# State-space stage and gate projections of a hybrid decoder block: order written by hand instead of chosen by the scheduler

## The chip, the cores and the metric

One core of a Trainium2 chip runs the whole program. The metric is the device time of one execution in microseconds (us). Five engines take part, each with its own in-order instruction stream: TensorE (PE, matrix products and transposes), VectorE (DVE), ScalarE (ACT), GpSimd (POOL) and SyncE (SP, DMA issues). Engines wait for one another on semaphores only, so an instruction that waits holds everything behind it on its own engine.

## The reference

One decoder block on 512 tokens of width 1024. After a norm, one projection gives the inputs of a state-space (S5) branch `u`, of a sparse-attention branch, and two sets of gate inputs `g_ssm`, `g_attn` (1024 columns each):

```python
xn = rmsnorm(h, norm1_g[layer])
proj = xn @ w_in[layer]
u, q, k, v, qi, ki, wi, g_ssm, g_attn = jnp.split(proj, offsets, axis=-1)
y_ssm = s5_branch(u, ...)          # y = Re(C * scan(a_bar, b_bar u)) + d_skip*u; gelu; glu
y_attn = dsa_branch(q, k, v, qi, ki, wi)
merged = (sigmoid(g_ssm) * (y_ssm @ w_ssm_up[layer])
          + sigmoid(g_attn) * (y_attn @ w_attn_up[layer]))
h = h + merged @ w_out[layer]
h = h + peer_ffn(rmsnorm(h, norm2_g[layer]), ...)
return rmsnorm(h, norm_f_g)
```

The state of S5 is a complex number per group and state, so its rotation by time step stands in tables of cosines and sines. `peer_ffn` takes most of the time and is not touched.

## The kernel before, in words

**Products.** A float32 product is made of three float32r products of high and low parts (`mmh`, L245 to L250: wH by xH, wH by xL, wL by xH). A weight half (4 of the 8 row blocks of 256 columns) comes by one DMA (SP) into `wraw`, ACT casts its two 128x512 pieces to `wH` (L87), and POOL (in places DVE) subtracts to get `wL` (L88). So each half costs two L87 on ACT, two L88 on POOL and 24 products of 512 columns on PE. **Gates:** 2048 gate columns are 16 halves, 384 products `mm<-xnH,wH` and the like (loop at L668 to L680 in before): for every 256 columns two PSUM banks `mm`, then two ACT copies `mg<-mm` (L679) and two DMAs to `sig_d` in memory, from where they are read again when the branches are merged.

**S5.** 16 column groups are done in two halves of NQ = 8, each in two groups of four. `s5_tables` makes per half: the tables Ex on DVE (four products of 128x512 and four block-diagonal 64x512 operations), whose transposes ("turns", L580) PE puts into a PSUM bank and ACT copies out (L581); the rotation tables Rc, Rs by doubling from a first column, which POOL sets by two small memsets (L583, L584), seven levels of six DVE operations; the F tables (L137 on 128x640 and 64x640); the Br copies (L605); and the "direct" products L612 with ACT copies L617. `s5_main` then makes the "enter" products L634, turns the result by Rc, Rs on DVE (six operations of 128x512 per group), runs 16 scans (L645, L646), turns back (six more), makes the "sums" L656 to L659 (12 small products per group), adds `hf<-sp,hf` on DVE, and ACT takes 16 gelus per group (L666) into `yf`. L137 is the line of the helper through which all DVE tensor-tensor operations go; `hf` is the name of every S5 work tile. PSUM banks for S5 are `sp` and `po` only.

**Order.** In before, S5 and the gates stand in plain program order, and the tile scheduler places every instruction: it puts S5 table work on DVE into the gaps of the attention stage, 51 gate products ahead of attention, and the rest around the S5 products where PE would wait. Everything from the transposes of the attention output on (L688, `pt<-ident,yt`; then `yaH`, attn_up, glu, ssm_up, w_out, PEER) is the same in both kernels.

Of the kernel before, what the change touches and what calls it, by code (L numbers as in the profile page):

```python
# [59 lines left out]
def block_kernel(ctx, tc, I, out):  # L60
# [75 lines left out]
    def tt(o, a, b, op, e=V):  # L136
        e.tensor_tensor(o, a, b, op=op)  # L137
        return o
# [66 lines left out]
    with ExitStack() as fr:  # L205
# [6 lines left out]
        def mmps(tag="mm"):  # L212
            return psm.tile([P, 512], F32, name=tag, tag=tag, bufs=1 if tag == "sp" else 2)

        def tps():
            return pst.tile([P, 4, P], F32, name="pt", tag="pt")
# [116 lines left out]
        with tc.tile_pool(name="s5", bufs=1) as fp:  # L333
# [213 lines left out]
            Tq = half([NQ, P], "Tq")  # L547
            for z in (Fr, Fi, Tq):
                G.memset(z, 0.0)

            def s5ps(tag):
                ps = pso.tile([P, 4, P], F32, name="po", tag="po") if tag == "po" else mmps("sp")
                return ps if tag == "po" else ps.rearrange("p (x c) -> p x c", x=4)

            def s5_tables(q0):
                qs = slice(q0, q0 + NQ)

                def bc_s(a, n=4):
                    return a[:, qs, None, :].to_broadcast([P, NQ, n, 16])

                def bc_c(a, n=4):
                    return a[:, qs, :, None].to_broadcast([P, NQ, n, 16])

                def blockdiag(dst, a, b, op):
                    for j in range(2):
                        ps_ = slice(64 * j, 64 * j + 64)
                        tt(dst[ps_, :, :, 16 * j:16 * j + 16], a[ps_], b[ps_], op)

                ETr, ETi = half([NQ, P], "ETr"), half([NQ, P], "ETi")
                v1, v2 = half([NQ, 4, 16], "vr"), half([NQ, 4, 16], "vi")  # L570
                for part, dst in ((0, ETr), (1, ETi)):
                    Ex = half([NQ, 4, 32], "B" if part else "A")
                    G.memset(Ex, 0.0)
                    tt(v1, bc_c(rev_r), bc_s(bbi if part else bbr), ALU.mult)
                    tt(v2, bc_c(rev_i), bc_s(bbr if part else bbi), ALU.mult)
                    blockdiag(Ex, v1, v2, ALU.add if part else ALU.subtract)
                    for q in range(0, NQ, 4):
                        pt = s5ps("po" if q0 and q else "sp")
                        for x in range(4):
                            PE.transpose(pt[:, x, :], Ex[:, q + x].rearrange("p a b -> p (a b)"), ident)  # L580
                        S.copy(dst[:, q:q + 4, :], pt)  # L581
                Rc, Rs = half([NQ, P], "Rc"), half([NQ, P], "Rs")
                G.memset(Rc[:, :, 0:1], 1.0)  # L583
                G.memset(Rs[:, :, 0:1], 0.0)  # L584
                r1, r2 = half([NQ, 64], "D"), half([NQ, 64], "yk")
                n = 1
                for m in range(2, 9):
                    bc = lambda a: a[:, qs, None].to_broadcast([P, NQ, n])
                    cmul(Rc[:, :, n:2 * n], Rs[:, :, n:2 * n], Rc[:, :, :n], Rs[:, :, :n],
                         bc(zr[m]), bc(zi[m]), r1[:, :, :n], r2[:, :, :n])  # L590
                    n *= 2
                v1, v2 = half([NQ, 5, 16], "vr"), half([NQ, 5, 16], "vi")
                tt(v1, bc_c(ap_r, 5), bc_s(cr_, 5), ALU.mult)
                tt(v2, bc_c(ap_i, 5), bc_s(ci_, 5), ALU.mult)
                blockdiag(Fr, v1, v2, ALU.subtract)
                tt(v1, bc_c(ap_r, 5), bc_s(ci_, 5), ALU.mult)
                tt(v2, bc_c(ap_n, 5), bc_s(cr_, 5), ALU.mult)
                blockdiag(Fi, v2, v1, ALU.subtract)
                Brs = []
                for src, tg in ((bbr, "C"), (bbi, "A")):  # L600
                    Br = half([NQ, 4, 32], tg)
                    G.memset(Br, 0.0)
                    for j in range(2):
                        ps_ = slice(64 * j, 64 * j + 64)
                        V.tensor_copy(Br[ps_, :, :, 16 * j:16 * j + 16],  # L605
                                      src[ps_, qs][:, :, None, :].to_broadcast([64, NQ, 4, 16]))
                    Brs.append(Br)
                for q in range(0, NQ, 4):
                    pt = s5ps("po" if q0 and q else "sp")
                    for x in range(4):  # L610
                        for Br, Fx in zip(Brs, (Fr, Fi)):
                            PE.matmul(pt[:, x, :], Br[:, q + x].rearrange("p a b -> p (a b)"),  # L612
                                      Fx[:, q + x, 0:4, :].rearrange("p a b -> p (a b)"),
                                      start=(Br is Brs[0]), stop=(Br is Brs[1]))
                    for s in range(4):
                        ps_ = slice(32 * s, 32 * s + 32)
                        S.copy(Tq[ps_, q:q + 4, 32 * s:], pt[ps_, :, :P - 32 * s])  # L617
                return ETr, ETi, Rc, Rs

            yf = at.tile([P, 4, T], F32, name="yf", tag="qT")  # L620

            def s5_main(q0, tabs, uk):
                ETr, ETi, Rc, Rs = tabs
                vr, vi = half([NQ, P], "vr"), half([NQ, P], "vi")
                groups = [slice(q, q + 4) for q in range(0, NQ, 4)]
                HHr, HHi = half([NQ, P + 1], "A"), half([NQ, P + 1], "B")
                x1, x2 = half([NQ, P], "C"), half([NQ, P], "D")
                V.memset(HHr[:, :, 0:1], 0.0)
                V.memset(HHi[:, :, 0:1], 0.0)
                for g, gq in enumerate(groups):  # L630
                    pr, pi = s5ps("sp"), s5ps("po")
                    for ET, ps in ((ETr, pr), (ETi, pi)):
                        for x in range(4):
                            PE.matmul(ps[:, x], ET[:, 4 * g + x, :], uk[:, q0 + 4 * g + x, :], start=True, stop=True)  # L634
                    tt(x1[:, gq], pr, Rc[:, gq], ALU.mult)
                    tt(vi[:, gq], pr, Rs[:, gq], ALU.mult)
                    tt(vr[:, gq], pi, Rs[:, gq], ALU.mult)
                    tt(x2[:, gq], pi, Rc[:, gq], ALU.mult)
                    tt(x1[:, gq], x1[:, gq], vr[:, gq], ALU.add)
                    tt(x2[:, gq], x2[:, gq], vi[:, gq], ALU.subtract)  # L640
                yk = half([NQ, P], "yk")
                for n_, g in enumerate(groups):
                    for q in range(g.start, g.stop):
                        rb = r4[:, q0 + q:q0 + q + 1].to_broadcast([P, P])
                        V.tensor_tensor_scan(vr[:, q], rb, x1[:, q], 0.0, op0=ALU.mult, op1=ALU.add)  # L645
                        V.tensor_tensor_scan(vi[:, q], rb, x2[:, q], 0.0, op0=ALU.mult, op1=ALU.add)  # L646
                    tt(x1[:, g], vr[:, g], Rc[:, g], ALU.mult)
                    tt(x2[:, g], vi[:, g], Rs[:, g], ALU.mult)
                    tt(HHr[:, g, 1:], x1[:, g], x2[:, g], ALU.subtract)
                    tt(x1[:, g], vi[:, g], Rc[:, g], ALU.mult)  # L650
                    tt(x2[:, g], vr[:, g], Rs[:, g], ALU.mult)
                    tt(HHi[:, g, 1:], x1[:, g], x2[:, g], ALU.add)
                    ps = s5ps("po" if n_ else "sp")
                    for x in range(4):
                        q = g.start + x
                        PE.matmul(ps[:, x], Tq[:, q, :], uk[:, q0 + q, :], start=True, stop=False)  # L656
                        PE.matmul(ps[:, x], Fr[:, q, 1:5, :].rearrange("p a b -> p (a b)"), HHr[:, q, :P],
                                  start=False, stop=False)
                        PE.matmul(ps[:, x], Fi[:, q, 1:5, :].rearrange("p a b -> p (a b)"), HHi[:, q, :P],  # L659
                                  start=False, stop=True)  # L660
                    yq, uq = yk[:, g], uk[:, q0 + g.start:q0 + g.stop]
                    tt(yq, uq, dsk[:, q0 + g.start:q0 + g.stop, None].to_broadcast([P, 4, P]), ALU.mult)
                    tt(yq, ps, yq, ALU.add)
                    for m in range(4):
                        for x in range(4):
                            S.activation(yf[32 * m:32 * m + 32, (q0 + g.start) // 4, x * P:x * P + P],  # L666
                                         yq[32 * x:32 * x + 32, m, :], AF.Gelu_apprx_tanh)

            for q0 in range(0, 16, NQ):
                s5_main(q0, s5_tables(q0), uk)  # L670


            for side in range(2):
                for c0 in range(0, D, 256):
                    pss = [mmps(), mmps()]
                    ch_chunk(win, 1576 + D * side + c0, xnH, xnL, pss)
                    for c in range(2):
                        sg = mtile()
                        S.activation(sg, pss[c], AF.Copy)  # L679
                        S.dma_start(sig_d[8 * side + c0 // P + c], sg)  # L680

        lt = fr.enter_context(tc.tile_pool(name="late", bufs=1))
        yaH = lt.tile([P, 4, T], F32R, name="yaH", tag="aH")
# [770 lines left out]
```

## Time and profile before

| | us |
|---|---|
| three runs | 1655.98, 1655.98, 1665.59 (median 1655.98) |
| the profiled execution, own time | 1661.05 |
| its span in the trace | 1659.3 |
| PE busy in the span | 1596.2 (96%) |
| DVE busy | 1327.2 (80%) |
| ACT busy | 701.1 (42%) |
| POOL busy | 702.9 (42%) |

The page gives busy time per engine over the whole span. PE is the bound of the program as a whole, by the PEER stages behind about 430 us; the change lies between about 125 us and 314 us, and there the rows by stage are what counts. "Busy" of PE comes from modelled ends of pipelined products: products that follow one another every 0.23 us are each shown as 0.39 us long. A row of the timeline has its start, its duration, the engine, the line, the tiles and, in brackets, the idle time before it and what ended it.

### The profile page before, as it was taken

The numbers are of one execution on the slowest core, as the hardware profiler recorded it, in microseconds if no ns is written. First come the engines' busy times: TensorE is split into PE (matmuls) and PEld (weight loads), VectorE is DVE, ScalarE is ACT, GpSimd is POOL, SyncE is SP. The second block draws the span as 40 slices with busy tenths as digits, with TensorE's granted clock in tenths as the row PEclk, the third lists the DMA queues.
The fourth block names the chain that finished last, engine by engine and source line by source line (L and its number), as shares of the span: only waits on it lengthen the run. The fifth ranks groups of instructions, "written<-read, shape, count | busy, mean of one in ns | idle before, by whom it ended". The sixth has DMA issues, their size and how long they took to land.

```text
span 1659.3 us, 24741 instructions
## 1 busy us (share of the span) xinstructions
PE 1596.2 (96%) x8942; PEld 1385.5 (84%) x8942; DVE 1327.2 (80%) x2743; ACT 701.1 (42%) x1216; POOL 702.9 (42%) x520
## 2 busy tenths in 40 slices
PE   6899978999999999999999999999999999999997
PEld 5886766789888999888898878888899999999986
DVE  6997798262579998998757788888778888888886
ACT  5536453553443355456543333333333333333334
POOL 4440141444334557654374233233344445544450
PEclk9999999999999999999999999999999999999999
DMA  6151022534523468876689999999999999999994
GB/s 192 45 147 39 26 85 81 165 127 155 166 93 111 139 206 322 293 244 241 257 288 330 375 366 351 377 378 315 308 340 339 357 338 345 364 330 353 356 326 171
DMA packets 183563, 408.15 MB, mean 246 GB/s; under 512 B 15441, under 2 KB 100993, under 8 KB 180369
## 3 DMA queue, kind: packets, MB, share of 16 engines
q1 hardware_dynamic: 136640, 224.37, 40.3%
q0 software_dynamic: 39168, 142.62, 24.2%
q10 hardware_dynamic: 7632, 39.59, 5.9%
q8 instruction: 70, 1.15, 0.3%
q14 instruction: 53, 0.43, 0.1%
HBM read 361.09 MB, written 45.44 MB: 245 GB/s over the span
## 4 chain that ended last, share of the span: by engine, by line
PE 62%; DVE 17%; DMA 3%; issue 3%; ACT 2%; POOL 1%; SPq 0%; DVEq 0%; ACTq 0%; POOLq 0%
PE acc L1310 9%; PE acc L1309 9%; PE acc L1308 9%; PE pu L99 8%; PE pu L101 8%; PE pu L100 7%; DVE hf L137 3%; PE pg L1076 2%; DMA raw<-peer_v 2%; DVE ti L874 1%; DVE rows L1121 1%; DVE pr L137 1%; DVE tv L872 1%; PE mm L248 1%; PE mm L249 1%
## 5 line engine op out<-in xcount | busy, mean ns | idle before, releaser
L99 PE MATMUL pu<-hnH,eH 128*128 128x368 f32 x1024 | 354.4, 346 | 0.0
L101 PE MATMUL pu<-hnH,eL 128*128 128x368 f32 x1024 | 337.6, 330 | 0.0
L100 PE MATMUL pu<-hnL,eH 128*128 128x368 f32 x1024 | 337.5, 330 | 0.0
L87 ACT CAST eH<-raw 128x1024 fp32r<-128x1024 f32 (+1 forms) x290 | 285.9, 992 | 109.1 <-PE acc L1310 49.2
L88 DVE TENSOR_TENSOR eL<-raw,eH 128x1024 fp32r<-128x1024 f32 x185 | 226.5, 1225 | 100.9 <-ACT eH L87 99.2
L1310 PE MATMUL acc<-eH,AL 128*128 128x512 f32 x768 | 305.6, 398 | 0.3 <-DVE AL L137 0.3
L1309 PE MATMUL acc<-eL,AH 128*128 128x512 f32 x768 | 302.7, 394 | 0.0
L1308 PE MATMUL acc<-eH,AH 128*128 128x512 f32 x768 | 301.6, 393 | 0.1
L88 POOL TENSOR_TENSOR eL<-raw,eH 128x1024 fp32r<-128x1024 f32 (+1 forms) x105 | 215.3, 2061 | 199.8 <-ACT eH L87 197.9
L826 POOL DMA_INDIRECT rows<-peer_v,eid x128 | 164.2, 1282 | 238.1 <-DVE acc0g L840 213.7
L826 POOL DMA_INDIRECT rows<-peer_u,eid x128 | 159.6, 1247 | 197.1 <-DVE rows L838 180.5
L88 POOL TENSOR_TENSOR wL<-wraw,wH 128x512 fp32r<-128x512 f32 (+1 forms) x90 | 127.6, 1442 | 188.6 <-ACT wH L87 188.6
L100 PEld LDWEIGHTS pu<-hnL,eH 128*128 128x128 f32 x1024 | 193.6, 189 | 2.5
L99 PEld LDWEIGHTS pu<-hnH,eH 128*128 128x128 f32 x1024 | 193.2, 189 | 2.7
L101 PEld LDWEIGHTS pu<-hnH,eL 128*128 128x128 f32 x1024 | 193.1, 189 | 0.0
L838 DVE SCALAR_TENSOR_TENSOR rows<-rows,hn 128x1024 f32<-128x1024 f32 x128 | 168.6, 1319 | 19.9 <-DMA rows<-peer_u,eid 19.8
L1310 PEld LDWEIGHTS acc<-eH,AL 128*128 128x128 f32 x768 | 144.2, 188 | 34.5 <-DVE AL L137 1.2
L1309 PEld LDWEIGHTS acc<-eL,AH 128*128 128x128 f32 x768 | 144.1, 188 | 34.3
L1308 PEld LDWEIGHTS acc<-eH,AH 128*128 128x128 f32 x768 | 144.2, 188 | 32.3 <-ACT AH L1294 0.5
L840 DVE SCALAR_TENSOR_TENSOR acc0g<-rows,dots,acc0g 128x1024 f32<-128x1024 f32 x128 | 163.9, 1280 | 8.6 <-DMA rows<-peer_v,eid 8.1
L1294 ACT CAST AH<-am 128x384 fp32r<-128x384 f32 x128 | 65.8, 514 | 246.4 <-DVE am L137 244.7
L804 ACT ACTIVATE hg<-pu 128x368 f32<-128x368 f32 x56 | 26.8, 478 | 152.5 <-PE pu L101 152.5
(396 smaller groups left out, 2727.8 us busy)
## 6 DMA issues: line engine op xcount, KB each, us to landing
raw<-uT SPq DMA_DIRECT2D x128, 512.0 KB
raw<-peer_v SPq DMA_DIRECT2D x128, 512.0 KB
g_d<-stg ACTq DMA_DIRECT2D x24, 1024.0 KB
gt<-g_d SPq DMA_DIRECT2D x16, 1536.0 KB
wraw<-w_in SPq DMA_DIRECT2D x26, 512.0 KB
hold_d<-hold ACTq DMA_DIRECT2D x13, 768.0 KB
hold<-hold_d SPq DMA_DIRECT2D x13, 768.0 KB
raw<-peer_wq SPq DMA_DIRECT2D x16, 512.0 KB
```

Of the source, the lines that this page charges most:

```text
L87: S.copy(H, src)
L88: e.tensor_tensor(L, src, H.bitcast(F32), op=ALU.subtract)
L99: PE.matmul(ps, wh, xh, start=first, stop=False)
L100: PE.matmul(ps, wh, xl, start=False, stop=False)
L101: PE.matmul(ps, wl, xh, start=False, stop=last)
L137: e.tensor_tensor(o, a, b, op=op)
L826: G.indirect_dma_start(out=r, out_offset=None, in_=I["peer_v"] if tab else I["peer_u"], in_offset=bass.IndirectOffsetOnAxis(ap=eid[:, j:j ...
L838: V.scalar_tensor_tensor(r, r, 1.0, hn0, op0=ALU.mult, op1=ALU.mult, accum_out=dj)
L840: V.scalar_tensor_tensor(acc0, r, dj, acc0, op0=ALU.mult, op1=ALU.add)
L1308: PE.matmul(o, AH[:, ts], H[:, cs], start=st, stop=False)
L1309: PE.matmul(o, AH[:, ts], L[:, cs], start=False, stop=False)
L1310: PE.matmul(o, AL[:, ts], H[:, cs], start=False, stop=sp)
```

## The change

S5 and gates go into a block in which the scheduler moves nothing: the order on each engine is the order in which the code emits. A small planner in the code keeps two clocks (`pe`, `dve`) with assumed costs (0.69 for three gate products, 0.9 per turn, 1.8 per enter or direct, 2.7 per sums, 0.09 + n/800 per DVE operation) and puts gate steps of three products between S5 products until the PE clock is 2 us past the time at which the operands should be ready. The S5 tables of a half now stand as one piece ahead of its main part, both adds of a half stand behind all its scans, four banks instead of two take S5 products (`sp`, `po`, `pt`, `pt`), and gate banks alternate between `mm` and `as`. Gate weights are loaded two halves ahead; gelus are kept in `later` and emitted when the PE clock has passed their time. The products, DVE operations and gelus themselves are the same in kind and number.

```diff
+            class Gates:
+                def load(self):
+                    if self.todo:
+                        c0, k0 = self.todo.pop(0)
+                        self.W.append(whalf(win, k0, c0, 256))
+                def run(self):
+                    for n in range(8):
+                        tag = "as" if n % 2 else "mm"
+                        pss = [mmps(tag), mmps(tag)]
+                        for hf in range(2):
+                            H, L = self.W.pop(0)
+                            for c in range(2):
+                                for k in range(4):
+                                    mmh(pss[c], [...], hf == k == 0, hf == 1 and k == 3)
+                                    yield
+                                if hf:
+                                    sg = mtile()
+                                    S.activation(sg, pss[c], AF.Copy)
+                                    S.dma_start(sig_d[2 * n + c], sg)
+                            self.load()
...
+            def product(t, cost, fn):
+                while now["pe"] < t + 2.0:
+                    while later and later[0][0] <= now["pe"]:
+                        later.pop(0)[1]()
+                    if next(dense.steps, dense) is dense:
+                        break
+                    now["pe"] += 0.69
+                now["pe"] = max(now["pe"], t) + cost
+                fn()
...
+            banks = ["sp", "po", "pt", "pt"]
...
                 Rc, Rs = half([NQ, P], "Rc"), half([NQ, P], "Rs")
                 G.memset(Rc[:, :, 0:1], 1.0)
                 G.memset(Rs[:, :, 0:1], 0.0)
...
+                    product(now["dve"] - 1.0, 1.8, direct)
...
+                def leave():
+                    for g, yq, t in outs:
+                        ps = s5ps()
...
+                        product(t, 2.7, sums)
+                        t_ = vt(yq, ps, yq, ALU.add, now["pe"] + 0.3)
...
+                        later.append((t_ + 0.5, active))
...
-            for q0 in range(0, 16, NQ):
-                s5_main(q0, s5_tables(q0), uk)
-            for side in range(2):
-                for c0 in range(0, D, 256):
-                    pss = [mmps(), mmps()]
-                    ch_chunk(win, 1576 + D * side + c0, xnH, xnL, pss)
...
+            for _ in range(2):
+                dense.load()
+            now["dve"] = 0.0
+            with tc.manual_schedule():
+                for q0 in range(0, 16, NQ):
+                    tables = s5_tables(q0)
+                    ins = s5_enter(q0, next(tables))
+                    Rc, Rs = next(tables)
+                    s5_main(q0, ins, Rc, Rs)()
+                while next(dense.steps, dense) is not dense:
+                    now["pe"] += 0.69
+                    while later and later[0][0] <= now["pe"]:
+                        later.pop(0)[1]()
+                for _, fn in later:
+                    fn()
```

**POOL, the queue from the first S5 memsets on.** L88 is the subtraction for a weight's low part; L583 and L584 (before) and L641 and L642 (after) set the first column of Rc and Rs, on which the doubling of the rotations starts. Before:

```order
L573 MEMSET hf 128x1024
L88 TENSOR_TENSOR wL<-wraw,wH 128x512 x2
L573 MEMSET hf 128x1024
L602 MEMSET hf 128x1024
L88 TENSOR_TENSOR wL<-wraw,wH 128x512 x24
L602 MEMSET hf 128x1024
L88 TENSOR_TENSOR wL<-wraw,wH 128x512 x6
L583 MEMSET hf 128x8
L584 MEMSET hf 128x8
```

After:

```order
L635 MEMSET hf 128x1024
L88 TENSOR_TENSOR wL<-wraw,wH 128x512 x20
L641 MEMSET hf 128x8
L642 MEMSET hf 128x8
L694 MEMSET hf 128x1024 x2
L88 TENSOR_TENSOR wL<-wraw,wH 128x512 x12
L635 MEMSET hf 128x1024 x2
L88 TENSOR_TENSOR wL<-wraw,wH 128x512 x2
L641 MEMSET hf 128x8
L642 MEMSET hf 128x8
```

In before the first half's column memsets stand ahead of the weight splits; in after those of the first half stand behind 20 splits, of which the last two belong to a gate half, and those of the second half behind a gate half's pair again.

**ACT, around the first half's gelus.** `mg<-as` copies a gate bank out, L672 copies a turn out, L762 is the gelu. After:

```order
L87 CAST wH<-wraw 128x512 x4
L762 ACT_TABLE_LOAD
L762 ACTIVATE yf<-hf 32x128 x32
L579 ACTIVATE mg<-as 128x512
L580 DMA sig_d<-mg 128x512
L579 ACTIVATE mg<-as 128x512
L580 DMA sig_d<-mg 128x512
L87 CAST wH<-wraw 128x512 x2
L672 COPY hf<-sp 128x512
L672 COPY hf<-po 128x512
L672 COPY hf<-pt 128x512 x2
```

In before the gelus of the two groups stood apart, 16 and 16, with a gate copy and a weight cast between them; in after all 32 of a half stand together, and the weight casts (L87) whose splits come ahead of the second half's L641 stand behind them.

**ACT, the end of the stage.** The gelus of the last groups, the casts `ys<-yf` of the S5 output and the casts `yaH<-pt` of the attention output, after:

```order
L762 ACTIVATE yf<-hf 32x128 x16
L87 CAST wH<-wraw 128x512 x2
L762 ACTIVATE yf<-hf 32x128 x16
L87 CAST wH<-wraw 128x512
L87 CAST ys<-yf 128x512
L579 ACTIVATE mg<-as 128x512
L87 CAST ys<-yf 128x512
L580 DMA sig_d<-mg 128x512
L87 CAST ys<-yf 128x512 x2
L579 ACTIVATE mg<-as 128x512
L87 CAST yaH<-pt 128x4x128
```

In before the same gelus and `ys` casts are followed by four more gate copies `mg<-mm` with their weight casts before the first `yaH`; in after two gate copies are left there. On PE the pieces move the same way: 102 gate products stood between the last sums and the transposes L688, 36 do now; 24 instead of 51 stand ahead of attention.

## Rows read from the trace of the kernel before

**Rows 1.** Busy time of each engine by stage (windows view, core 0).
```profile
core 0: us, PE busy (x) PEld busy (x) DVE busy (x) ACT busy (x) POOL busy (x), PEclk, DMA share, GB/s
66.00:125.00 59.00, 55.99 (x338) 49.03 (x337) 58.91 (x182) 18.37 (x37) 24.76 (x19) 1.00 0.44 126
125.00:183.00 58.00, 57.13 (x327) 39.74 (x328) 44.99 (x214) 34.49 (x103) 3.53 (x3) 0.97 0.09 27
183.00:287.00 104.00, 84.82 (x471) 69.17 (x471) 92.33 (x167) 41.93 (x99) 32.00 (x24) 0.98 0.24 73
287.00:314.00 27.00, 24.45 (x110) 19.44 (x108) 6.08 (x6) 17.72 (x40) 12.57 (x9) 1.00 0.54 179
```
**Rows 2.** PE's waits, 183 to 313 us: total us, times, longest.
```profile
PE sp L657 <- DVE hf L137: 4.1, 2, 2.3
PE sp L612 <- DVE hf L137: 3.1, 2, 2.0
```
**Rows 3.** DVE's waits in the same stretch.
```profile
DVE hf L137 <- PE po L659: 4.7, 2, 4.0
```
**Rows 4.** DVE's timeline: the end of attention, the last S5 add.
```profile
181.82 0.69 DVE L137 TENSOR_TENSOR yt<-po,sums 128x512 f32<-128x512 f32 x1 [1.50 <-PE po L433]
...
286.63 0.69 DVE L137 TENSOR_TENSOR hf<-po,hf 128x512 f32<-128x512 f32 x1 [4.01 <-PE po L659]
```
**Rows 5.** PE's timeline: last sums' start, gate products behind the last sums, first attn_up product.
```profile
284.19 0.38 PE L659 MATMUL po<-hf 128*128 128x128 f32 x2
...
286.34 0.47 PE L250 MATMUL mm<-xnH,wL 128*128 128x512 f32 x1
...
311.74 0.39 PE L249 MATMUL mm<-xnL,wH 128*128 128x512 f32 x1
311.97 0.39 PE L250 MATMUL mm<-xnH,wL 128*128 128x512 f32 x1
...
316.51 0.74 PE L248 MATMUL mm<-yaH,wH 128*128 128x512 f32 x2 [0.67 <-ACT yaH L87]
```
**Rows 6.** Operations on S5 tiles in the attention stage: DVE's sum, then groups (ns min/median/max).
```profile
125.00:183.00 58.00, 20.75 (x56) 0.97 0.09 27
...
L137 DVE TENSOR_TENSOR hf<-hf x17: 169/284/690, 139.8 to 179.0; 64x512 f32<-64x512 f32 x4, 128x8 f32<-128x8 f32 x2, 128x16 f32<-128x16 f32 x2, 128x32 f32<-128x32 f32 x2
L137 DVE TENSOR_TENSOR hf<-sm,s_br x2: 418/419/420, 157.1 to 162.6; 128x256 f32<-128x256 f32 x2
...
L137 DVE TENSOR_TENSOR hf<-rev_r,bbr x1: 689/689/689, 165.5 to 165.5; 128x512 f32<-128x512 f32 x1
...
L137 DVE TENSOR_TENSOR hf<-ap_r,s_cr x1: 821/821/821, 178.1 to 178.1; 128x640 f32<-128x640 f32 x1
```
**Rows 7.** POOL by line, 183 to 287 us: count, busy us, mean ns, idle.
```profile
L88 POOL TENSOR_TENSOR wL<-wraw,wH 128x512 fp32r<-128x512 f32 x18 | 28.1, 1579 | 52.9 <-ACT wH L87 52.9
```
**Rows 8.** POOL's timeline: a pair of splits beside DVE, a single one.
```profile
210.84 3.65 POOL L88 TENSOR_TENSOR wL<-wraw,wH 128x512 fp32r<-128x512 f32 x2 [4.43 <-ACT wH L87]
...
274.02 1.27 POOL L88 TENSOR_TENSOR wL<-wraw,wH 128x512 fp32r<-128x512 f32 x1 [5.59 <-ACT wH L87]
```
**Rows 9.** DVE's timeline: the same operation beside a split and without one.
```profile
211.66 1.69 DVE L137 TENSOR_TENSOR hf<-hf 128x512 f32<-128x512 f32 x1
...
216.21 0.66 DVE L137 TENSOR_TENSOR hf<-hf 128x512 f32<-128x512 f32 x1
```
**Rows 10.** ACT's timeline: gelus, turn copies, weight casts, last casts of the stage.
```profile
232.41 0.59 ACT L581 COPY hf<-sp 128x512 f32<-128x512 f32 x1
...
287.35 5.10 ACT L666 ACTIVATE yf<-hf 32x128 f32<-32x128 f32 x16 [1.64 <-DVE hf L137]
292.48 0.60 ACT L679 ACTIVATE mg<-mm 128x512 f32<-128x512 f32 x1
...
294.14 1.14 ACT L87 CAST ys<-yf 128x512 fp32r<-128x512 f32 x2
...
313.23 0.58 ACT L87 CAST yaH<-pt 128x512 fp32r<-128x512 f32 x1
```

## What the time will be

> **What bounds the kernel now.** The page gives PE as the bound of the whole program, but the change lies in four stages, so I read busy time by stage first [rows 1]. Up to 125 us DVE has no room (58.91 of 59 us busy). In attention, to 183 us, PE has none (57.13 of 58). From 183 to 287 us, the S5 stage, neither is full: DVE 92.33 of 104, PE 84.82. From 287 to 314 us PE works off the rest of the gates. PE's waits say who is late in the S5 stage: sums and direct products waiting for DVE [rows 2]. DVE in turn waits longest for the very last sums, 4.0 us [rows 3], after which it has nothing to do in S5. So in before DVE sets the pace to 287 us and then PE does, with 102 gate products behind the last sums: they run from 286.34 to 312.2 us [rows 5]. At 316.51 us attn_up starts, and from there on both kernels run the same instructions on PE. A shift of that start is the change in time.
>
> **What PE gains.** Between 183 and 314 us PE is busy 84.82 + 24.45 = 109.3 of 131 us and idle 21.7. The changed kernel leaves 27 more gate products to this stretch (24 instead of 51 ahead of attention). One follows another in 0.23 us [rows 5], so that is 6.1 us more work. Nearly all 27 come out of the DVE-bound stage before 125 us, where they cost nothing; I count four inside attention, and taking these out lets attention end 0.9 us earlier. If PE then never waited, its stretch would end 21.7 - 6.1 + 0.9 = 16.5 us earlier. That is the most the change can give by this way.
>
> **What DVE must do.** DVE ends attention at 182.5 us and its last S5 add at 287.3 [rows 4]. Of these 104.8 us it works 92.33 + 0.9 (what lies outside the stage's window) = 93.2 and waits 11.6. Now its work grows. In attention it did 20.75 us of S5 work in gaps [rows 6]. Of this stay there: four Ex products of 0.69, four block-diagonal operations of 0.69 (the longest of their group), and the input matrix (four of 0.42 and two near 0.4): 8.0 us. The first half's rotations and two F products (0.82 each) go behind attention, as the emitted order has them: 20.75 - 8.0 = 12.8 us. They were hidden under a full PE; now nothing hides them. Without a single wait and with as many disturbances as before, DVE would end at 182.5 - 0.9 + 93.2 + 12.8 = 287.6, the same time as now. All that removing DVE's waits can give is used up by moving the rotations.
>
> **What is added to it.** Four terms:
>
> First, the wait for the first column. The doubling starts on a column that POOL sets, now behind a gate half's two splits, which stand behind their casts on ACT, which stand behind the copy of a turn. From the end of attention: copy 0.59 [rows 10], one cast 0.57 (half of the pair of 1.14), two splits of 1.27 each [rows 8]: 3.7, and 0.5 for the turn, 4.2 us. Some of it can lie before attention ends. I take 3.5, between 0 and 4.5.
>
> Second, the same in the second half, but behind gelus. From the first add on: 32 gelus 10.2, two gate copies 1.2, one cast 0.57, two splits 2.54 (sizes from [rows 8, 10]), 14.5 us to the memset. Meanwhile DVE waits some 1.5 us for the second sums, adds (0.69) and makes Ex (5.5): 7.7. The rest, 6.8, is a wait in which DVE has nothing: in its program the rotations come next. Behind DVE there wait F, Br, the direct products and all mains. I take 7; below 0 it cannot go, and above lies 9 if the copies wait for their gate products.
>
> Third, the adds. Both stand behind all scans, and the second one waits for its 12 products. Before, the last sums took from 284.19 to 286.34 us [rows 5], 2.2 us, while DVE has one add (0.69) to do: 1.5 us in each half, 3.0 us. In before the first add was hidden by the second group's scans. Between 1 and 4.
>
> Fourth, splits. A 128x512 operation that takes 0.66 us alone took 1.69 beside a split of POOL [rows 9], the split in the pair 1.83 instead of 1.27 [rows 8]: 1.03 us lost on DVE for each. The S5 stage had 18 of them [rows 7]; after, 14 halves of gate weights are cast and split behind attention and ahead of the last sums, since weights come two halves ahead: 28. Of the ten more, I take six to fall into DVE's waits (two ahead of each column memset, two in the waits at adds), so four by 1.03: 4.1 us, between 0 and 10.3.
>
> In the Trainium skill, page "SBUF — State Buffer", section "Who interferes with whom", a DVE instruction with two SBUF inputs contends with a GpSimd instruction that reads SBUF, as one holder at a time. Rotations have two SBUF inputs, so moving them out of attention, where POOL is busy 3.53 us, to where it splits weights speaks against this change. With a lock held for the split's whole 1.27 us the four would cost 5.1 instead of 4.1 us; the trace agrees with the rule in kind and shows somewhat less per split.
>
> DVE's last add is then at 287.6 + 3.5 + 7 + 3.0 + 4.1 = 305.2 us.
>
> **The tail.** Before, the last 16 gelus began at 287.35 us and were hidden by gate products; the `yaH` casts stood at 313.23 [rows 10]. Now 32 gelus come together. The first add is 1.5 + 0.7 us ahead of the second, so they start at 303.0; 32 take 10.2, a pair of casts between them 1.1: 314.3. Then come a cast 0.5, four `ys` casts 2.1 and two gate copies 1.2: the first `yaH` at 318.1 instead of 313.23, +4.9 us. PE, with only 36 gate products (8.2 us) behind the last sums, is ready before that: the cover of the gelus is gone. attn_up shifts by the same 4.9 us, from 316.5 to 321.4. Added to the profiled execution's own 1661.05 that is 1666; the runs' median is 5 us below this execution, so by it 1655.98 + 4.9 = 1661 us.
>
> **The rivals.**
>
> A: PE is the bound and the planner's cover works. For it: PE waits sum to 21.7 us, and gate steps in threes fit into them; four banks let it run ahead. It would need DVE's waits gone. With the first two terms and the splits at 0 and the adds at 1, DVE ends at 288.6, and the same 12.9 us from its last add to `yaH` give 301.5. PE has 109.3 + 6.1 - 1.8 (at most, what lies behind 312.2 is transposes) from 182.1 us on, to 295.7, and with some 3 us at the sums it ends near 299, so `yaH` rules: -11.7 us, 1644 us. Against it: the two column memsets stand in POOL's queue as written.
>
> B: the weights come late (slower). The casts ahead of the second column memset need their weights; if these are not there, the 6.8 us wait grows one for one, and all DVE work of the second half with it. It decides from 6.8 + 11.7 = 18.5 us of wait, when the whole is over 1% slower; with 20 us the time is 1655.98 + 4.9 + 13.2 = 1674 us. Against it: DMA engines are busy 0.24 of the stage [rows 1], and a load leaves two halves, 48 products or 11 us of PE, ahead.
>
> C: the change of order does nothing to the end. DVE was done at 287.3 us and PE at 312.2, 25 us of slack; if DVE's four terms come out at 13 instead of 17.6 us, its growth of 13 and the longer tail just fill that slack, and the first `yaH` stands where it stood: 0 to +1 us, 1656. For it: two of the terms rest on how POOL and ACT interleave, and may be smaller. Against it: each of them has its instructions in the emitted order.
>
> A lower clock is a doubt at both ends: the granted clock was 0.98 of full speed in the S5 stage and 0.97 in attention [rows 1], with PE at work 0.82 of the time in S5. With fewer gate products ahead of attention and longer PE waits at the sums it may fall once more, but while DVE sets the pace this lies beside it; 2 us at most in the tail.
>
> **How the numbers follow.** 1% is 16.6 us, about what a measurement of this kernel can tell from no change. Forecast (DVE chain with the tail) 0.55, with about 1655 to 1667 as its own range. C 0.13. A 0.20, a third of it beyond 1%, if the sums wait less than I give them and attention ends earlier still. B, with the upper ends of the four terms (305.2 + 1 + 2 + 1 + 6.2 = 315.4, so +15.1 us, 1671), 0.12, two thirds beyond 1%. Faster: 0.07 from A and 0.03 for a gain in attention that these rows do not show, 0.10. Slower: 0.08 from B and 0.04 from the forecast's own tail, 0.12. Within 1%: 0.78. The range reaches to A below, 1643, and to the upper ends above, 1672.
>
> **What would show it.** Right: attention's last DVE operation near 181 to 182 us, then a DVE gap of some 3 us before the first small rotation and one of some 7 us in the second half, both ended by POOL's memset; 32 gelus in a row; PE idle in front of the last transposes. The first term is wrong if the first rotation follows attention at once; the second if the memset L641 is done before Ex ends; the fourth if no more DVE operations of two SBUF inputs show 1 us on top beside a split than before. The tail is wrong if gate products still run when `yaH` starts. The whole is wrong if PE has fewer than 10 us idle from 183 us to the transposes.

## The result and the profile after

The changed kernel takes 1705.45 us (three runs, 1704.0 to 1706.29), the one before 1655.98 (1655.98 to 1665.59): 1.0275 times as long, with a 95% interval of 1.0252 to 1.0298 (the two medians alone stand at 1.030, since two of the three runs of before gave 1655.98). It is 2.75% slower; the prediction was 1661 us with a range of 1643 to 1672. The profiled execution of after has a span of 1703.7 us and a mean granted clock of 0.964 of full speed, before 0.992. (Some executions of e1 and e2 below ended 30 to 40 us later than the others of the same kernel; they are told there, since their cause is the subject here.)

Busy time by stage of the kernel after; it answers [rows 1], with the same columns.

```profile
core 0: us, PE busy (x) PEld busy (x) DVE busy (x) ACT busy (x) POOL busy (x), PEclk, DMA share, GB/s
66.00:125.00 59.00, 51.61 (x317) 45.38 (x315) 58.87 (x190) 16.43 (x35) 18.14 (x14) 0.97 0.38 108
125.00:183.00 58.00, 57.54 (x182) 37.56 (x180) 25.53 (x140) 20.98 (x71) 0.00 (x0) 0.50 0.00 1
183.00:240.00 57.00, 52.76 (x272) 41.05 (x271) 36.67 (x74) 20.28 (x42) 17.86 (x14) 0.91 0.20 57
240.00:287.00 47.00, 39.87 (x219) 35.14 (x220) 36.30 (x70) 23.16 (x57) 14.50 (x14) 0.89 0.22 67
287.00:314.00 27.00, 19.90 (x89) 16.18 (x87) 26.12 (x45) 7.40 (x13) 10.03 (x7) 0.91 0.50 156
314.00:411.00 97.00, 88.24 (x399) 73.52 (x400) 53.95 (x82) 50.82 (x104) 35.73 (x26) 0.92 0.36 117
```

The row to look at is the second. PE is shown as busy as before (57.54 of 58 us), but the granted clock is 0.50 (1.2 GHz) where it was 0.97, and 182 matmul records stand where there were 327. A PE column alone would not have shown it. PE's timeline ahead of attention and inside it, in after:

```profile
118.23 0.39 PE L250 MATMUL mm<-xnH,wL 128*128 128x512 f32 x1
124.33 1.00 PE L447 MATMUL as<-kT,qT 64*128 64x128 f32 x4 [5.71 <-DVE mx L450]
...
183.52 2.07 PE L447 MATMUL as<-kT,qT 64*128 64x512 f32 x2
...
191.07 1.12 PE L447 MATMUL as<-kT,qT 64*128 64x512 f32 x2
```

The 24 gate products end at 118.6 us; PE then has nothing until DVE's `mx` is there, 5.71 us, and no gate product stands inside attention. But for four scores that ran at 112.5 us, attention starts at the low clock and stays there: its scores of 64x512 take 2.07 us for a pair at 183.5 us, and 1.12 us only from about 190 us on.

DVE's timeline in after: the last operation of attention, the first rotation of each half, the second add of each half. It answers [rows 3, 4].

```profile
206.10 0.69 DVE L137 TENSOR_TENSOR yt<-po,sums 128x512 f32<-128x512 f32 x1 [2.53 <-PE po L433]
211.80 0.25 DVE L137 TENSOR_TENSOR hf<-hf,sm 128x8 f32<-128x8 f32 x2 [5.01 <-POOL hf L642]
...
269.16 0.69 DVE L137 TENSOR_TENSOR hf<-pt,hf 128x512 f32<-128x512 f32 x1 [1.39 <-PE pt L754]
283.44 0.26 DVE L137 TENSOR_TENSOR hf<-hf,sm 128x8 f32<-128x8 f32 x2 [8.07 <-POOL hf L642]
...
341.42 0.69 DVE L137 TENSOR_TENSOR hf<-pt,hf 128x512 f32<-128x512 f32 x1 [4.05 <-PE pt L754]
```

From these rows, those of ACT below and [rows 4, 5, 10], the loss in order of time:

| from, to | before | after | difference |
|---|---|---|---|
| start to the end of DVE's last attention operation | 182.5 | 206.8 | +24.3 |
| to the end of the last S5 add | 104.8 | 135.3 | +30.5 |
| to the first `yaH` cast | 25.9 | 10.9 | -15.0 |
| to the first attn_up product | 3.3 | 4.2 | +0.9 |
| to the end of the span | 1342.8 | 1346.5 | +3.7 |

The sum is 44.4 us, between the two profiled executions (the medians differ by 49.5, with before at 1655.98; in later measurements its median was 1660.6 to 1661.3). The prediction had -0.9, +18.8 and -13.0 in the first three lines and nothing in the last two, so the largest part that it did not have stands in the first line. In the last line some 1.4 us are an estimate from the first 20 us of attn_up, whose granted clock is 0.93 in after and 1.00 in before; the rest is spread over 1300 us.

POOL's and ACT's timelines of after at the second half's column memsets and at the end of the stage:

```profile
280.86 2.49 POOL L88 TENSOR_TENSOR wL<-wraw,wH 128x512 fp32r<-128x512 f32 x2 [10.05 <-ACT wH L87]
283.29 0.11 POOL L641 MEMSET hf<- 128x8 f32 x1
```

```profile
267.81 10.22 ACT L762 ACTIVATE yf<-hf 32x128 f32<-32x128 f32 x32 [11.11 <-DVE hf L137]
278.05 0.60 ACT L579 ACTIVATE mg<-as 128x512 f32<-128x512 f32 x1
...
280.16 1.14 ACT L87 CAST wH<-wraw 128x512 fp32r<-128x512 f32 x2 [0.45 <-ACT mg L579]
...
352.97 0.58 ACT L87 CAST yaH<-pt 128x512 fp32r<-128x512 f32 x1
```

The queue is as it was read from the order: 32 gelus, two gate copies, two casts, two splits, and only then a memset of 0.11 us for which DVE waits 8.07 us.

### The profile page after: what moved, and what is told of

It is laid out like the page before. It is cut to its first block, busy times and chain, and to the rows that moved or that the text cites. A ratio compares the mean times of both kernels' runs of the same rounds, so it can differ in the third digit from the quotient of the medians.

```text
span 1703.7 us, 24731 instructions
## 1 busy us (share of the span) xinstructions
PE 1632.0 (96%) x8942; PEld 1414.0 (83%) x8942; DVE 1335.9 (78%) x2743; ACT 701.9 (41%) x1216; POOL 703.4 (41%) x520
## 4 chain that ended last, share of the span: by engine, by line
PE 62%; DVE 6%; issue 4%; DMA 4%; POOL 2%; ACT 1%; SPq 0%; DVEq 0%; ACTq 0%; POOLq 0%
PE acc L1411 9%; PE acc L1410 9%; PE acc L1409 9%; PE pu L99 8%; PE pu L101 7%; PE pu L100 7%; PE pg L1177 2%; DMA rows<-peer_v,eid 2%; PE pg L200 2%; PE pg L201 2%; PE pg L202 2%; POOL rows L927 1%; DMA raw<-peer_v 1%; DVE rows L1222 1%; PE px L1100 1%
## 5 line engine op out<-in xcount | busy, mean ns | idle before, releaser
L87 ACT CAST eH<-raw 128x1024 fp32r<-128x1024 f32 (+1 forms) x290 | 286.0, 992 | 107.1 <-PE acc L1411 51.5
L88 DVE TENSOR_TENSOR eL<-raw,eH 128x1024 fp32r<-128x1024 f32 x185 | 226.5, 1224 | 96.2 <-ACT eH L87 95.9
L88 POOL TENSOR_TENSOR eL<-raw,eH 128x1024 fp32r<-128x1024 f32 (+1 forms) x105 | 215.4, 2062 | 199.4 <-ACT eH L87 198.4
L88 POOL TENSOR_TENSOR wL<-wraw,wH 128x512 fp32r<-128x512 f32 (+1 forms) x90 | 127.6, 1442 | 274.0 <-ACT wH L87 274.0
```

Of the source, the lines that this page charges most:

```text
L87: S.copy(H, src)
L88: e.tensor_tensor(L, src, H.bitcast(F32), op=ALU.subtract)
```

## The experiments

Each kernel was timed against the kernel before on the same chip; that one had medians of 1660.6 to 1661.3 us there, so ratios are given beside times.

**Is the lost clock a matter of the products ahead of attention? 48 instead of 24 (e1).**

```diff
             with tc.manual_schedule():
+                for _ in range(8):
+                    next(dense.steps)
                 for q0 in range(0, 16, NQ):
```

> The changed kernel with 24 more gate products (48 instead of 24) ahead of attention; 24 fewer stand at the end, all else in the changed order. Clock theory (PE sat idle 5.7 us from 118.6 to 124.3 us, the granted clock fell to 0.50, and attention's own small products did not bring it back until 188 us): the gap closes to under 1 us, the clock of 125 to 183 us is near 1.0, attention's last DVE operation comes at about 182 to 184 us instead of 206.1, and the time is 1705 - 23 = about 1682 us. Rival (attention is slower because the fixed S5 order takes DVE and ACT from it): attention still ends near 206 us, 1705 us.

Three of six executions took 1674.2 to 1677.1 us (ratio 1.0097, 1.0064 to 1.0129), three 1706.6 to 1715.2. The profile caught one of the latter. In it PE works until 125.5 us and then idles 1.40 us:

```profile
126.86 0.70 PE L447 MATMUL as<-kT,qT 64*128 64x128 f32 x4 [1.40 <-DVE mx L450]
```

The last five of the 48 gate products stand behind this idle time, inside attention, from 127.49 to 130.26 us. The clock goes like this:

```profile
125.00:130.00 5.00, 3.60 (x13) 2.08 (x12) 4.30 (x29) 2.13 (x5) 0.00 (x0) 0.77 0.29 106
131.00:134.00 3.00, 2.81 (x16) 1.88 (x15) 2.11 (x18) 2.37 (x12) 0.00 (x0) 0.99 0.00 0
135.00:183.00 48.00, 48.00 (x142) 29.95 (x141) 18.03 (x96) 16.52 (x52) 0.00 (x0) 0.50 0.00 1
```

It falls, comes back for 3 us, and falls for nearly all the rest of attention, which ends at 217.8 us. So 48 products put attention on an edge: to judge by the times, it kept the clock in half of the executions; in the profiled one it did not.

**The same with products that nobody reads, no gate product moved (e2).**

```diff
+                fill = mmps("sp")
+                for j in range(24):
+                    PE.matmul(fill, dense.W[0][0][:, j % 4, :P], xnH[:, j % 4, :], start=True, stop=True)
```

> The changed kernel with 24 products of the same 512 columns, whose results nobody reads, put ahead of attention; no gate product is moved. Clock theory: the same as for 48 gate products, attention ends near 182 to 184 us, 1682 us, since only PE's being at work matters. Rival (it is which gate work stands where, the weights loaded with it and the queues behind it): no gain, 1705 to 1711 us.

1675.08 us, the median of four; three took 1674.1 to 1675.5 (ratio 1.0088, 1.0057 to 1.0120), one 1704.2. The profile has attention at full clock and its last DVE operation 27.5 us earlier than after:

```profile
125.00:183.00 58.00, 55.79 (x331) 39.60 (x332) 36.11 (x171) 34.66 (x102) 1.80 (x2) 1.00 0.00 1
```

```profile
178.58 0.69 DVE L137 TENSOR_TENSOR yt<-po,sums 128x512 f32<-128x512 f32 x1 [2.63 <-PE po L433]
```

It is PE's being at work, not which gate work stands there. The profile has an idle time of 1.40 us ahead of attention here too, and five gate products behind it; the clock stayed at 1.00 through both.

**The converse: the kernel before, all but 24 gate products held behind attention (e4).** Its scheduler orders the rest; `last["pv"]` is attention's last product on PE.

```diff
+                        after = tc.issue_after(last["pv"].ins)
+                        if side or c0 or hf: after.__enter__()
...
```

> The kernel before, with all but the first 24 gate products held behind attention's last product on TensorE; its scheduler orders everything else. Clock theory: PE idles about 5 us ahead of attention, the clock falls to 0.50 for most of it, attention ends near 205 us instead of 182.5, and the time is 1656 + 23 + up to 6 us of products that now come later = 1680 to 1686 us. Rival (the loss in attention comes from the fixed order): attention ends at 182 us, the time is 1656 to 1662 us.

1693.36 us (ratio 1.0219, 1.0174 to 1.0264). Without any of the fixed order PE idles 5.70 us ahead of attention, no gate product stands inside it, and the stage is as in after; the last `yt` operation starts at 205.92 us:

```profile
125.00:183.00 58.00, 57.54 (x180) 37.69 (x180) 26.12 (x168) 21.52 (x71) 0.00 (x0) 0.50 0.01 2
```

```profile
205.92 0.69 DVE L137 TENSOR_TENSOR yt<-po,sums 128x512 f32<-128x512 f32 x1 [0.95 <-PE po L433]
```

In this profile the first `yaH` comes at 342.27 us, 29.0 later than in before: 24.1 of it is attention, 4.9 the gates held back, as the expectation's sum had it (23 and up to 6). The median's rise over the kernel before, 32.5 us, is 3.5 more; the four executions spread from 1689.0 to 1702.9, and why is not known.

**Idle time left alone, 24 unread products inside attention (e11).**

```diff
+                    if i == 0 and h == 5:
+                        with tc.issue_after(qk.ins):
+                            fill = mmps("sp")
+                            for j in range(24):
+                                PE.matmul(fill, xnH[:, j % 8, :P], xnH[:, j % 8, :], start=True, stop=True)
```

> The changed kernel with its idle time ahead of attention left as it is, and 24 unread products of 512 columns inside attention, behind its first few heads. If what is lacking is work that raises the clock (attention's own small products hold it at best), the clock comes back to 1.0 during these 24 (some 8 us at the low clock) and stays; attention ends at about 189 us instead of 206 and the time is about 1688 us. Rival (the length of the idle time decides for the whole stage, or attention's own products pull the clock down again at once): the 24 products are only added, attention ends at 212 us or later, 1710 us and over.

1685.67 us (ratio 1.0137, 1.0113 to 1.0161). The clock comes back while these 24 run, and attention's own products hold it to the end:

```profile
125.00:130.00 5.00, 4.53 (x17) 3.33 (x18) 3.99 (x35) 2.88 (x14) 0.00 (x0) 0.50 0.00 0
130.00:135.00 5.00, 5.00 (x22) 4.23 (x21) 4.31 (x31) 0.78 (x4) 0.00 (x0) 0.79 0.01 2
150.00:183.00 33.00, 33.00 (x192) 22.35 (x191) 16.28 (x42) 18.33 (x47) 0.00 (x0) 1.00 0.00 0
```

```profile
186.31 0.69 DVE L137 TENSOR_TENSOR yt<-po,sums 128x512 f32<-128x512 f32 x1 [2.82 <-PE po L433]
```

Work added to PE made the program 20 us faster. The idle time takes the clock away; after it, attention's own small products do not bring it back before its 64x512 scores at 189 us, and the 24 wide ones do.

**48 gate products and 8 unread ones (e5).** One edit on e1: eight products as in e2, behind the 24 gate products that e1 puts first.

> The changed kernel with 48 gate products ahead of attention and 8 more unread products behind them, so that PE is at work (1.8 us) through the 1.4 us idle time at attention's second pair of products, which 48 alone leave. If it is that idle time that decides whether attention runs at 2.4 or 1.2 GHz, every execution is like the better ones of 48 alone: 1674 to 1677 us, attention's end near 180 us. Rival (attention's own products drop the clock in some executions whatever stands ahead): executions at 1705 us and over still occur.

1675.37 us (1672.2 to 1677.0; ratio 1.0080, 1.0060 to 1.0099), with none of four executions late. The time is as expected, the path is not: the eight stand at 118.88 us among the gate products, and PE idles 1.40 us as in e1. What has moved is what stands behind the idle time, eight gate products instead of five:

```profile
124.74 0.70 PE L447 MATMUL as<-kT,qT 64*128 64x128 f32 x4 [1.40 <-DVE mx L450]
...
130.44 0.48 PE L248 MATMUL mm<-xnH,wH 128*128 128x512 f32 x1
```

With eight there, none of the 41 executions of e5 to e10 took more than 1677.1 us; with five there, three of six (e1) and one of four (e2) were late. The profiles of e6 and e8 show the fall itself: the clock goes to 0.50 behind an idle time of 1.4 us, is back at 1.00 by 132 us, when seven of the eight have run, and holds. In e6:

```profile
128.00:129.00 1.00, 1.00 (x4) 0.76 (x4) 0.97 (x8) 0.00 (x0) 0.00 (x0) 0.50 0.00 0
140.00:183.00 43.00, 42.39 (x258) 29.43 (x257) 32.98 (x142) 23.85 (x63) 0.00 (x0) 1.00 0.02 7
```

So the idle time alone, which e5's expectation made the cause, does not decide. That the number of wide products behind it does is what these traces suggest; no run changed that number alone. The loss in attention, 30.1 us, is gone with e5; what is left belongs to the S5 stage. The next kernels build on e5.

**The first columns on VectorE, in after (e3) and on e5 (e6).**

```diff
-                G.memset(Rc[:, :, 0:1], 1.0)
-                G.memset(Rs[:, :, 0:1], 0.0)
+                V.memset(Rc[:, :, 0:1], 1.0)
+                V.memset(Rs[:, :, 0:1], 0.0)
```

> The changed kernel with the first columns of the rotation tables set by VectorE instead of GpSimd; nothing else. Queue theory: the two waits of DVE for POOL (5.0 and 8.1 us) go, and since DVE is the chain through the state-space stage the time falls by 9 to 13 us, to about 1694 us. Rival (something else is as late, so the waits reappear at the next step, or the weight splits now fall beside DVE operations): 0 to -4 us, 1701 to 1705 us. The clock in attention stays at 0.50 in both.

> The same with the rotation tables' first columns set by VectorE. Queue theory: as it took 10 us off the changed kernel (1705.5 to 1695.4), it takes 8 to 10 us off here: 1665 to 1668 us. Rival (10 us were partly a change of the clock): under 4 us, 1671 us and over.

e3: 1695.42 us (ratio 1.0215, 1.0190 to 1.0240), 10.0 less than after. e6: 1664.1 us (ratio 1.0016, 1.0000 to 1.0032), 11.3 less than e5. The two waits, 13.1 us in after, go. But that is not all of the gain: with the column on DVE, the doubling of the first half starts before attention ends, and 6.4 us of S5 work go back into attention's gaps (14.2 us there in e3 and e6, 7.8 in after). Some of the waiting is met again at the next step, as DVE's timeline of e3 shows, first row the start of the doubling, then the second half (the wait for ACT's gelus to free a tile, then for the sums, which had been 4.05):

```profile
196.09 0.25 DVE L137 TENSOR_TENSOR hf<-hf,sm 128x8 f32<-128x8 f32 x2
...
270.47 0.17 DVE L137 TENSOR_TENSOR hf<-hf,sm 128x8 f32<-128x8 f32 x1 [2.39 <-ACT yf L762]
...
329.61 0.69 DVE L137 TENSOR_TENSOR hf<-pt,hf 128x512 f32<-128x512 f32 x1 [5.28 <-PE pt L754]
```

**The splits (e8).** e6, with the high part used in place of the low part from the third weight half on, so 28 splits on GpSimd are left out.

> The kernel with columns set by VectorE, but from the third weight half on the gates' low parts are not computed (the high parts are used in their place, so the gates are wrong): 28 splits of GpSimd fall away, the products and casts stay. If splits beside DVE operations cost about 1.03 us each and 20 of them hit the DVE chain, the time falls by some 10 to 20 us against the kernel with columns alone. If it is only the four that the prediction counted: 4 us.

1652.55 us (ratio 0.9941, 0.9918 to 0.9964), 11.5 less than e6. With attention ending at the same time (182.8 and 182.9 us), the last S5 add starts at 294.29 instead of 307.60 us: 13.3 us for 28 splits, 0.48 us each on the chain, where a split beside a DVE operation costs 1.03. DVE's own work on S5 tiles from attention's end to the last add fell by more (e6, then e8; length of the stretch, DVE busy, then clock and DMA):

```profile
182.81:308.29 125.48, 107.47 (x178) 0.95 0.34 105
182.86:294.98 112.12, 88.02 (x178) 0.99 0.38 118
```

That is 19.5 us for 26 splits fewer in this stretch (30 and 4), 0.75 each. DVE waits 6.1 us more instead, ahead of the first scans above all: 11.5 us where e6 has 5.0, until 215.5 us in both. `HHr`, which is set there, takes the buffer of a Br copy that PE's direct products read until 215.4 us (215.5 in e8), and these stand behind gate products. So in the first half PE took back what DVE gained.

**The first half's tables back into attention (e7).** e6, with Ex, rotations and F of the first half emitted ahead of the fixed block.

```diff
+            first = list(s5_tables(0))
+            now["dve"] = 0.0
             with tc.manual_schedule():
...
-                    tables = s5_tables(q0)
+                    tables = iter(first) if q0 == 0 else s5_tables(q0)
```

> The same again with the first half's tables (Ex, rotations, F) emitted ahead of the fixed block, so that the scheduler puts their DVE operations into the gaps of attention, as in the kernel before. If DVE is the chain and the moved rotations cost their 12.8 us, the time falls by 10 to 13 us, to about 1654 us. Rival (PE or the weight splits set the end of the stage by then, or attention gets longer by the work put into it): 0 to -5 us, 1660 to 1667 us.

1661.35 us (ratio 1.0004, 0.9992 to 1.0017): 2.7 less than e6, not 10 to 13. DVE's chain did shrink, from 125.5 us between attention's end and the last add to 113.8, but only 4.9 of these 11.7 us are work moved (107.5 to 102.6 us): e6 already had half of the first half's tables in attention. The rest are waits, the 5.0 us ahead of the first scans above all. The gain went to PE: with DVE's planner clock set back, fewer gate products were placed ahead of the sums, and 66 (12 in e6) stand behind them until 308 us, before the transposes.

```profile
291.94 0.69 DVE L137 TENSOR_TENSOR hf<-pt,hf 128x512 f32<-128x512 f32 x1 [3.74 <-PE pt L754]
307.90 0.39 PE L250 MATMUL as<-xnH,wL 128*128 128x512 f32 x1
309.97 0.58 ACT L87 CAST yaH<-pt 128x512 fp32r<-128x512 f32 x1
```

From the last add to `yaH` it is 17.3 us here, in e6 7.5. (Of the two profiled executions e6's was among the slowest of its ten and e7's the fastest; the medians are what counts for the time.)

**The planner's slack (e9).** e7 with the constant 2.0 in `product` set to 4.0, which moves gate products ahead of the S5 products.

> The kernel with tables in attention, and the planner's slack at 4.0 instead of 2.0 us, so that some 20 gate products that stood behind the last sums (until 307.9 us, when the S5 chain had been done with at 292.6) stand ahead of the first sums and direct products, where PE waited 4.5 and 5.4 us. If the tail of gate products sets the end there, the first yaH cast comes 3 to 6 us earlier (304 to 307 us) and the time is 1656 to 1659 us against 1661.4. Rival (the products now delay S5 products that DVE waits for): the last add moves later by as much, no gain.

1656.75 us (1651.4 to 1657.1; ratio 0.9954, 0.9933 to 0.9976). The first `yaH` comes at 302.63 us, 7.3 earlier, with the last add 0.7 us later than in e7. PE's waits between 180 and 330 us in e9 (total, times, longest):

```profile
PE pt L754 <- DVE hf L137: 4.8, 3, 2.5
PE pt L796 <- DVE yaL L88: 3.7, 1, 3.7
PE sp L716 <- DVE hf L137: 2.5, 1, 2.5
```

This is the fastest version with the full product, and it beats before by a little: 0.46% by the ratio, 0.26% by the two medians (1656.75 and 1660.99).

**Each group's sums and add at its own place (e10).** e9 with `sums` right behind a group's scans and its add behind the next group's scans.

> The same, with the sums of a group right behind its own scans and its add behind the scans of the next group, as in the kernel before, so that the first group's 16 gelus run under the second group's work. If the adds at the end of a half cost what their waits show (3.9 and 3.7 us) and the gelus in one row 5 us at the end, the last add and the first yaH cast come 5 to 8 us earlier, 1651 to 1655 us. Rival (PE, out of gate products behind the last sums, idles and its clock falls for attn_up and glu): 1657 us and over.

1658.03 us (ratio 0.9976, 0.9960 to 0.9993), no gain over e9. The last add did not come earlier but at 300.15 us, 7.5 later than in e9, after a wait of 6.10 us for its sums: the last 36 gate products now stand ahead of these, from 288.39 to 297.3 us, though DVE was done at 294.05. The planner had no gate products left behind the last sums; PE stands still there and its clock falls for the start of attn_up:

```profile
297.00:302.00 5.00, 4.20 (x34) 3.65 (x33) 0.69 (x1) 2.71 (x7) 3.36 (x3) 1.00 0.70 221
302.00:307.00 5.00, 0.00 (x0) 0.00 (x0) 0.39 (x1) 4.83 (x15) 0.00 (x0) 0.63 0.30 94
307.00:312.00 5.00, 3.68 (x12) 2.99 (x13) 4.59 (x8) 3.21 (x7) 0.00 (x0) 0.50 0.26 105
```

## Why the prediction was wrong

**The step that failed** is in the part on PE: "Nearly all 27 come out of the DVE-bound stage before 125 us, where they cost nothing." They were what kept PE at work up to attention, and the last of them inside it: of the 51, eight stand behind attention's second scores (the prediction counted four, at 0.9 us). Without them the idle time grew from 1.41 to 5.71 us, nothing wide followed it, the clock fell and stayed low, and attention, which the prediction let end 0.9 us earlier, ended 24.3 us later. The rows for this stood in the trace of before, in PE's timeline at the start of attention, and were not drawn on:

```profile
125.81 0.70 PE L447 MATMUL as<-kT,qT 64*128 64x128 f32 x4 [1.41 <-DVE mx L450]
126.44 0.62 PE L249 MATMUL mm<-xnL,wH 128*128 128x512 f32 x1
...
130.16 0.39 PE L249 MATMUL mm<-xnL,wH 128*128 128x512 f32 x1
```

```profile
128.00:130.00 2.00, 2.00 (x6) 1.46 (x6) 0.36 (x4) 0.00 (x0) 0.00 (x0) 0.50 0.00 0
134.00:183.00 49.00, 48.94 (x294) 33.90 (x293) 38.85 (x166) 30.34 (x85) 3.53 (x3) 1.00 0.06 17
```

PE idles for 1.41 us, the products of 512 columns then take 0.62 instead of 0.39 us (granted clock 0.50), and after a few gate products inside attention they take 0.39 again and the clock holds. The prediction had the doubt ("with fewer gate products ahead of attention ... it may fall once more") and priced it at "2 us at most in the tail", because it asked only who sets the pace in S5. In attention PE is the bound (57.13 of 58 us busy), and the clock is paid there: from its second scores to the end of its last `yt` it takes 54.0 us in e2 at 1.00, 82.5 in after, where the clock is back from 190 us on, and 91.0 in e1's profile. e2, e4 and e11 show cause and size: with the clock held the changed kernel is 30 us faster, and holding back the products in the kernel before costs 32.5.

**What DVE must do** was the right chain: its sum gave 123.6 us from attention's end to the last add, after took 135.3, and with the clock held (e2) 133.7. The moved tables are what was said: DVE does 20.3 us of S5 work in attention in before and 7.8 in after, so 12.5 moved, 12.8 forecast. DVE's work from attention's end to the last add, before and after, in the same columns as for e8:

```profile
182.51:287.32 104.81, 93.14 (x167) 0.98 0.24 73
206.79:342.11 135.32, 112.85 (x208) 0.90 0.29 89
```

Its four terms:

- First column: 3.5 forecast, 5.0 waited. Second half: 7 forecast, 8.1. Both by the path that was named; without it e3 and e6 are 10 to 11 us faster, part of which is work that went back into attention.
- Adds: 3.0 forecast, 1.4 and 4.1 waited, 5.4. In the second half the sums' operands were made by 336.2 us, but PE worked off gate products until 338.5 and only then ran the sums, at a granted clock of 1.00. The term counted the sums alone, from a row misread: in before the last sums had begun at 280.61 us, not 284.19, and eight gate products stand among them.

```profile
338.54 0.38 PE L751 MATMUL pt<-uk,hf 128*128 128x128 f32 x2
```

- Splits: 4.1 forecast for ten more (18 to 28, as counted). DVE's work grew by 19.7 us; 12.5 of it moved, which leaves 7.2 for the ten, if nothing else changed; by e8's 0.75 us each they would be 7.5. So the choice that only four of the ten meet DVE was too small; the 1.03 us for one that does is not at odds with it.

Of DVE's 11.7 us over the sum, 5.0 are these waits, 2.8 work (3.1 at the splits, 0.3 less moved), and the other 3.9 idle time in pieces, 1.0 of it ahead of the scans, that the sum did not have.

**The tail**: 12.9 us forecast from the last add to `yaH`, 10.9 measured, PE idle ahead of the last transposes as said (3.9 us). The 32 gelus came in a row of 10.22 us in the first half and in two rows of 16 at the end.

For the kernel with its clock held the forecast of 4.9 us stands against about 14.8 for e5 (1675.4 over 1660.6): within 1%, as its chances had it, but too small by the terms above.

**Rivals.** A (PE the bound, waits gone) fell: the waits on POOL were real. e9, with the queue mended and the tables back in attention, is 4.2 us faster than before, where A had 11.7. B (weights late) did not happen; the casts ahead of the second memsets waited for nothing but ACT's own order. C fell with the sum. No rival had PE's clock in attention in it, and that was the event.

## What to carry to other kernels

Filler products on TensorE do two jobs: they use idle time, and they hold the clock for the stage behind them. Before filler is moved away from in front of a stage that PE bounds with small products, or out of it, look at the granted clock there and price that stage at the low one (here 54 us became 82 to 91). A memset of 0.1 us is as late as the queue it stands in (8.07 us here): set such a column on the engine that needs it. And a planner that fills PE's gaps can make PE late itself: in after, e6, e8 and e10 gate products stood ahead of S5 products for which DVE was waiting.

## What the hardware showed that was not expected

PE shown busy 57.5 of 58 us by its column ran at 1.2 GHz from 125 to 183 us (after and e4), and the same products held 2.4 GHz in e2, and in e11 once wide products had run. The Trainium skill's page "TensorE: Matmul & The Clock Gate", Part 1, has the clock set by how busy PE has been recently, and calls the number of products that run at the low clock at a start run-variable; the traces agree in kind: an idle time of 1.40 us ahead of attention left the clock at 1.00 in e2's profile, took it for about 4 us in before, and for all but some 3 us of attention in e1's. Where it was taken, gate products inside attention brought it back: eight of them for good (before, e6, e8), five for 3 us (e1's profile). Why the same idle time takes the clock in one profile and not in another was not found.
